# A decoder block in split fp32 on one core: residual tiles asked for earlier, a sum weighted ahead of its norm factor, conditioning sums moved one step on

## Chip, cores and metric

The kernel runs on one core of one Trainium2 chip. The metric is device microseconds of one execution, input in HBM to output in HBM.

## What is computed

One hybrid decoder block on x (1 x 1024 x 1024, float32). The reference, cut to the part that the change touches:

```python
ada = c_act @ w_ada[l] + b_ada[l]
sh1, sc1, gt1, sh2, sc2, gt2 = [a[:, None, :] for a in jnp.split(ada, 6, axis=-1)]
...
y = jax.nn.sigmoid(g_attn) * a + jax.nn.sigmoid(g_conv) * cv
x = x + gt1 * (y @ w_out[l])

h2 = rmsnorm(x, norm2_g[l]) * (1.0 + sc2) + sh2
fg, fu = jnp.split(h2 @ w_ffn_in[l], 2, axis=-1)
x = x + gt2 * ((jax.nn.silu(fg) * fu) @ w_ffn_out[l])
return rmsnorm(x, final_g)
```

## The kernel before

Activations are kept transposed, 128 channels on the partitions, in tiles of 128 x 1024 tokens, split into two token halves of 512 (`HB`). Every float32 operand of a matmul is split into a high part (rounded, written by ScalarE) and a low part (source minus high, made by VectorE), and a product is three matmuls: high x high, high x low, low x high. Three stages matter here.

**Output projection** (`wo`, L1116, 16 steps: eight channel tiles of the first token half, then eight of the second). Each step splits the next weight (`wh_wo` on ScalarE, `wl_wo` on VectorE, called through `low`), runs 24 matmuls into a bank, adds the result, weighted, to the residual tile `x1_m` on VectorE, stores that half to `x1_d` from POOL's queue (L1136), and squares it for the second norm. Beside this, VectorE makes the conditioning columns (`ada_step`, L272): a row tile of `w_ada` is fetched by SP (L269) into one of two buffers, multiplied by the condition vector and summed into one column of `cols` by a custom instruction. `AW` says how many are done in which step. Here a planner orders the instructions of TensorE, VectorE and ScalarE; behind the last step `in_order` fixes the program's own order.

**Transition into the feed-forward input.** The feed-forward products use Strassen's scheme: seven products per pair of hidden tiles (`Pair.PRODUCTS`), whose activations are A11, A12, A22 and the sums S1 to S4, and whose weights are B11, B22, B21, B12 and the differences T1 to T4. A11 and A12 are the first token half and are made during the projection. A21 and A22 are the second half and wait for the factor `rstd` of the second norm (`Norm2.stat`, L1076): ln and exp on ScalarE. For each of four channel tiles j, `scale1` (L1363) multiplies two tiles by weight and factor, adds them, has ScalarE write the high half of S1 with the two shifts added (`bsum`), and has ScalarE add the shift to each of the two tiles; `low1` makes the low half. `sums` makes S2 and leaves S3 in place, `sum4` makes S4, `blocks` splits S3 and A22. The first two pairs (`two`) run product by product side by side: 0, 5, 1, 2, 3, 4, 6; `both` (L1345) splits their weight blocks, and `evacuations` moves a finished bank out.

**Feed-forward output.** After the 22 pairs come `Group`s (L1268): the same seven products with three k-blocks each, whose activations (`gb`, 512 KB each) were stored to `gs_d` and come back through POOL's queue (`fetch_blocks`, L1466, issue L1476). Each product is added at once from its bank to the residual tile `x1r`, which `x1r()` (L1479, issue L1483) fetches from `x1_d` through SP's queue. SP's queue also carries the weight loads: L1176 for pairs, L1285 for Groups, two tiles each (`rawg` or `rawu`), and is served strictly in order. A slot for `gb` or `x1r` comes free when its last reader is done. The second product uses another bank than the first; the third uses the first's again.

```python
                if i == NFF - 1:
                    fetch_blocks(0, GP)
                    if p >= 5:
                        x1r()
```

## Time and profile before

| | us |
|---|---|
| runs (median, lowest, highest of 3) | 1387.37, 1385.5, 1387.46 |
| the profiled execution | 1386.32 |
| its span | 1384.6 |
| TensorE busy | 1333.0 |
| VectorE busy | 1063.5 |
| ScalarE busy | 637.0 |

The span is what the profile records of the execution; 1.7 us lie around it. The mean granted clock of TensorE is 0.994 of full speed. Times in the rows count from the start of the span. Busy time of TensorE is modelled from the starts of its matmuls, so gaps between them say more than its share.

### The profile page before, as it was taken

Reading aid. Unit: us, or ns where it says so; the run is one execution under the profiler, and the core shown is the slowest. Engines: PE = TensorE matmul, PEld = TensorE weight load, DVE = VectorE, ACT = ScalarE, POOL = GpSimd, SP = SyncE. Lnnn points to the kernel's source line nnn. Section 1 sums busy time; section 2 is a strip of 40 time slices with the busy share of each in tenths; the row PEclk is TensorE's granted clock in tenths of the full one; section 3 lists DMA queues with packets and bytes.
Section 4 is the critical chain, followed back from the end, with each engine's and each line's share of the span. In section 5 each row is a group of like instructions: output and inputs, shape, how many; then the busy total and the mean of one; then the engine's idle time right before and its main releaser. Section 6 shows DMA issues by size and latency. Waiting matters only on the chain.

```text
span 1384.6 us, 16471 instructions
## 1 busy us (share of the span) xinstructions
PE 1333.0 (96%) x6070; PEld 1090.8 (79%) x6070; DVE 1063.5 (77%) x1698; ACT 637.0 (46%) x1079; POOL 102.5 (7%) x181
## 2 busy tenths in 40 slices
PE   7899999999999999999997999999999997999997
PEld 5678887877788887788775888888888886888886
DVE  6847688889989897796789577877777765777764
ACT  5536667675611113732476454444444441222346
POOL 0000000000000000000100011111000031112004
PEclk9999999999999999999999999999999999999999
DMA  8610010100111122428721255554544499577213
GB/s 287 210 31 31 32 46 16 47 16 31 46 46 49 43 76 91 138 91 312 261 81 68 85 182 183 167 167 154 173 145 151 153 323 408 167 283 286 98 31 123
DMA packets 58899, 184.43 MB, mean 133 GB/s; under 512 B 6425, under 2 KB 11457, under 8 KB 58818
## 3 DMA queue, kind: packets, MB, share of 16 engines
q1 hardware_dynamic: 38242, 110.49, 24.3%
q0 software_dynamic: 20000, 72.36, 14.7%
q8 instruction: 48, 0.79, 0.2%
q10 hardware_dynamic: 576, 0.52, 0.1%
q14 instruction: 33, 0.27, 0.1%
HBM read 139.83 MB, written 43.52 MB: 132 GB/s over the span
## 4 chain that ended last, share of the span: by engine, by line
PE 77%; DVE 10%; ACT 6%; DMA 5%; issue 2%; SPq 0%; POOL 0%; DVEq 0%; ACTq 0%; POOLq 0%
PE fx L113 22%; PE fz L113 11%; PE proj L113 8%; PE ga L113 5%; PE fy L113 5%; PE gc L113 4%; PE wo L125 3%; PE oa L113 3%; PE oc L125 3%; PE fo L125 3%; DMA ada<-in_w_ada 2%; PE vacc L125 2%; PE sc L113 2%; PE av L113 2%; DMA gb<-gs_d 1%
## 5 line engine op out<-in xcount | busy, mean ns | idle before, releaser
L113 ACT ACTIVATE wbp<-tt 128x512 fp32r<-128x512 f32 (+1 forms) x75 | 43.9, 586 | 156.8 <-DVE tt L113 151.0
L113 DVE SCALAR_TENSOR_TENSOR cacc<-u,vec,cacc 128x1022 f32<-128x1022 f32 (+28 forms) x87 | 110.2, 1267 | 2.2
L113 PE MATMUL proj<-hhi,wh_in 128*128 128x512 f32 x239 | 98.3, 411 | 1.7 <-DVE kl L125 1.7
L113 PE MATMUL proj<-hhi,wl_in 128*128 128x512 f32 x240 | 93.9, 391 | 0.0
L113 PE MATMUL proj<-hlo,wh_in 128*128 128x512 f32 x240 | 93.6, 390 | 0.0
L113 ACT ACTIVATE wb<-tt 128x512 fp32r<-128x512 f32 (+1 forms) x59 | 35.4, 602 | 93.3 <-DVE tt L113 86.5
L113 PE MATMUL fx<-A,wb 128*128 128x512 f32 x299 | 70.9, 391 | 2.8 <-DVE g L113 2.8
L113 PE MATMUL fx<-S,wbp 128*128 128x512 f32 x276 | 67.1, 391 | 1.4 <-DVE S L113 1.3
L113 PEld LDWEIGHTS fx<-A,wb 128*128 128x128 f32 x299 | 56.0, 188 | 15.3 <-issue 3.7
L113 PE MATMUL fz<-S,wbp 128*128 128x512 f32 x276 | 66.5, 390 | 1.5 <-ACT S L113 1.3
L113 PE MATMUL fx<-gb,wbp 128*128 128x512 f32 x270 | 66.0, 390 | 0.3 <-DMA gb<-gs_d 0.3
L113 PE MATMUL fz<-S,wb 128*128 128x512 f32 x252 | 61.0, 390 | 1.6 <-DVE S L113 1.6
L113 PEld LDWEIGHTS fx<-S,wbp 128*128 128x128 f32 x276 | 51.6, 188 | 13.5 <-DVE S L113 2.5
L113 PE MATMUL fx<-S,wb 128*128 128x512 f32 x252 | 60.8, 390 | 1.4 <-DVE S L113 1.3
L113 PEld LDWEIGHTS fz<-S,wbp 128*128 128x128 f32 x276 | 51.7, 188 | 12.9 <-ACT S L113 1.7
L113 PEld LDWEIGHTS fx<-gb,wbp 128*128 128x128 f32 x270 | 50.5, 188 | 11.4 <-DMA gb<-gs_d 0.9
L125 ACT ACTIVATE e<-sc,mn 128x512 f32<-128x512 f32 (+7 forms) x64 | 47.2, 739 | 26.8 <-DVE mn L125 25.8
L113 DVE SCALAR_TENSOR_TENSOR x1r<-fx,cols,x1r 128x512 f32<-128x512 f32 x48 | 36.0, 750 | 30.2 <-PE fx L113 20.9
L113 PEld LDWEIGHTS fz<-S,wb 128*128 128x128 f32 x252 | 47.1, 188 | 12.2 <-DVE S L113 2.4
L113 PEld LDWEIGHTS fx<-S,wb 128*128 128x128 f32 x252 | 47.2, 188 | 11.9 <-DVE S L113 1.6
L113 DVE TENSOR_TENSOR wbp<-tt,wbp 128x512 fp32r<-128x512 f32 (+1 forms) x75 | 47.0, 628 | 11.7 <-ACT wbp L113 11.6
L113 PEld LDWEIGHTS proj<-hhi,wh_in 128*128 128x128 f32 x239 | 45.0, 188 | 11.1 <-issue 3.6
(354 smaller groups left out, 3603.8 us busy)
## 6 DMA issues: line engine op xcount, KB each, us to landing
gb<-gs_d POOLq DMA_DIRECT2D x57, 512.0 KB, 9.8
gs_d<-gstw POOLq DMA_DIRECT2D x36, 512.0 KB, 3.5
ada<-in_w_ada SPq DMA_DIRECT2D x32, 512.0 KB, 4.2
gs_d<-gst POOLq DMA_DIRECT2D x27, 512.0 KB, 4.3
rawu<-in_w_fi SPq DMA_DIRECT2D x22, 512.0 KB, 3.6
rawg<-in_w_fi SPq DMA_DIRECT2D x22, 512.0 KB, 4.5
adac<-in_w_ada SPq DMA_DIRECT2D x16, 512.0 KB, 5.2
wr_wo<-in_w_out SPq DMA_DIRECT2D x16, 512.0 KB, 5.0
```

Source lines behind the costliest of these rows:

```text
L113: self.last = f(*args, **kw)
L125: self.last = self.chain(f, *args, **kw) if self.chain else f(*args, **kw)
```

## The change

1. In the last pair, two x1r tiles are requested in the step of its first product, ahead of the rest of the first Group's `gb` blocks, of which that step asks for one and not three; before, they were requested in the steps of products 5 and 6.
2. S1 is formed from terms that are weighted before the factor is known: ScalarE weights A22's tile in place (`weigh22`: two tiles in the last projection step, two after the factor's instructions), VectorE adds the weighted A21 (`weigh1`: j = 0, 1 ahead of the factor). After the factor one multiplication per j remains ahead of the high half (`scale1`). S2 comes in one instruction from the sum, S3 in two from the unscaled tile, A22 in one multiplication by the factor, with the shift added on ScalarE (`sum22`) and again in the low half (`low22`). The T3 and T4 differences and the loads of pairs 2 and 3 move ahead of the first product. The low halves of T3 and T4 are no longer made by VectorE: ScalarE writes minus the high half, and an accumulating transfer from POOL's queue adds the source. The evacuations of product 0 move behind S1, the first pair's evacuation of product 4 ahead of A22. The factor gets a slot of its own.
3. The conditioning sums of a projection step are called in the next step, behind the low part of the next weight.

```diff
-                self.r = rstd_from([st], 1.0 / D, self.last)[0]
+                self.r = rstd_from([st], 1.0 / D, self.last, None if self.one else slot)[0]
...
             low()
+            if i:
+                ada_step(fx[0], AW[(i - 1) // KD][(i - 1) % KD], OCH)
             ps = bank("wo")
...
             norms[hf].add(m)
-            ada_step(fx[0], AW[hf][m], OCH)
             if hf:
                 for j in range(WA[m], WA[m + 1]):
                     apply0(j)
+            if i == 2 * KD - 1:
+                for j in range(KH - 2):
+                    weigh22(j)
...
-            def low(self, part):
+            def low(self, part, dma=False):
                 w, src = part
                 n = self.n
+                if dma:
+
+                    A.activation(w[:, n:2 * n], w[:, :n].bitcast(F32), AF.Copy, scale=-1.0)
+                    G.dma_start(w[:, n:2 * n], src, accum_op=ALU.add)
+                    return
...
+        def weigh22(j):
+
+            a22s.append(x1[KH + j][:, HB:])
+            A.activation(a22s[j], a22s[j], AF.Copy, scale=col(4, KH + j))
+
+        def weigh1(j):
+
+            if j % 2 == 0:
+                wide.append(slot(f"s1_{j}"))
+            sums1.append(wide[-1][:, hf_sl(j % 2)])
+            V.scalar_tensor_tensor(out=sums1[j], in0=x1[j][:, HB:], scalar=col(4, j), in1=a22s[j], op0=ALU.mult,
+                                   op1=ALU.add)
+
         def scale1(j):
-
-            for m in (j, KH + j):
-                norms[1].scale(m)
+            if j >= KH - 2:
+                weigh1(j)
+            t = sums1[j]
+            V.tensor_tensor(out=t, in0=t, in1=norms[1].r, op=ALU.mult)
             acts["S1"][j] = slot(f"S1_{j}", F32R)
-            t = sums1[j] = two[j % 2].t[:, HB:]
-            V.tensor_tensor(out=t, in0=x1[j][:, HB:], in1=x1[KH + j][:, HB:], op=ALU.add)
             A.activation(acts["S1"][j][:, :HB], t, AF.Identity, bias=bsum[:, j:j + 1])
-            for m in (j, KH + j):
-                norms[1].shift(m)
...
+        def sum2(j):
+
+            t = sums1[j]
+            V.scalar_tensor_tensor(out=t, in0=t, scalar=bsum[:, j:j + 1], in1=x1[j][:, :HB], op0=ALU.add,
+                                   op1=ALU.subtract)
+            high("S2", j, t)
+
+        def sum3(j):
+
+            norms[1].scale(j)
+            a21 = x1[j][:, HB:]
+            V.scalar_tensor_tensor(out=a21, in0=x1[j][:, :HB], scalar=col(3, j), in1=a21, op0=ALU.subtract,
+                                   op1=ALU.subtract)
+            high("S3", j, a21)
+
+        def sum22(j):
+            t = a22s[j]
+            V.tensor_tensor(out=t, in0=t, in1=norms[1].r, op=ALU.mult)
+            acts["A22"][j] = slot(f"A22_{j}", F32R)
+            A.activation(acts["A22"][j][:, :HB], t, AF.Identity, bias=col(3, KH + j))
...
         both(6, 7, 8, 9)
+        for j in range(KH - 2):
+            weigh1(j)
+        for t in ("T3", "T4"):
+            for g in two:
+                g.source(t)
+        pairs[2].load()
+        pairs[3].load()
         two[0].product(0)
         norms[1].stat()
+        for j in range(KH - 2, KH):
+            weigh22(j)
         two[1].product(0)
-        evacuations(0)
...
         staged(scale1, low1)
+        both(10, 11, dma=True)
+        evacuations(0)
         products(1)
         new_block("S2")
-        staged(sums, lambda j: low("S2", j, x1[j][:, :HB]))
+        staged(sum2, lambda j: low("S2", j, sums1[j]))
...
+        both(12, 13, dma=True)
         evacuations(2)
         products(3)
...
-        both(12, 13)
-        blocks("A22", lambda j: x1[KH + j][:, HB:])
-        evacuations(4)
+        two[0].evacuate(4)
+        new_block("A22")
+        staged(sum22, low22)
+        two[1].evacuate(4)
...
                 if i == NFF - 1:
-                    fetch_blocks(0, GP)
-                    if p >= 5:
+                    if p == 0:
+
                         x1r()
+                        x1r()
+                    fetch_blocks(0, GP if p else 1)
```

What this moves, at three places. First SP's queue around the last pair and the first Group, before:

```order
L1285 DMA rawg<-in_w_fo 128x768 x2
L1285 DMA rawu<-in_w_fo 128x768 x2
L1285 DMA rawg<-in_w_fo 128x768
L1483 DMA x1r_8893<-x_d 128x1024
L1483 DMA x1r_8911<-x_d 128x1024
L1483 DMA x1r_8973<-x_d 128x1024
L1483 DMA x1r_9005<-x_d 128x1024
L1285 DMA rawg<-in_w_fo 128x768
```

and now:

```order
L1294 DMA rawg<-in_w_fo 128x768 x2
L1294 DMA rawu<-in_w_fo 128x768
L1524 DMA x1r_8773<-x_d 128x1024
L1524 DMA x1r_8775<-x_d 128x1024
L1294 DMA rawu<-in_w_fo 128x768
L1294 DMA rawg<-in_w_fo 128x768 x2
L1524 DMA x1r_8979<-x_d 128x1024
L1524 DMA x1r_9011<-x_d 128x1024
```

Two x1r requests stand between the two `rawu` loads now, ahead of the `rawg` loads behind which all four stood; the other two stand behind the second of those.

Second VectorE around the factor (`wbp` are weight blocks, `small_78` holds the summed shifts, `cols_90` the weights and shifts), before:

```order
L113 TENSOR_TENSOR wbp_5576<-rawg_5497,wbp_5576 128x512
L113 TENSOR_TENSOR wbp_5578<-rawu_5501,wbp_5578 128x512
L113 SCALAR_TENSOR_TENSOR x1_0_4878<-x1_0_4878,cols_90,rstd_5601 128x512
L113 SCALAR_TENSOR_TENSOR x1_4_5037<-x1_4_5037,cols_90,rstd_5601 128x512
L113 TENSOR_TENSOR tt_5515<-x1_0_4878,x1_4_5037 128x512
L113 SCALAR_TENSOR_TENSOR x1_1_4919<-x1_1_4919,cols_90,rstd_5601 128x512
L113 SCALAR_TENSOR_TENSOR x1_5_5075<-x1_5_5075,cols_90,rstd_5601 128x512
L113 TENSOR_TENSOR tt_5520<-x1_1_4919,x1_5_5075 128x512
L113 SCALAR_TENSOR_TENSOR S1_0_5649<-tt_5515,small_78,S1_0_5649 128x512
```

and now:

```order
L113 TENSOR_TENSOR wbp_5578<-rawg_5497,wbp_5578 128x512
L113 TENSOR_TENSOR wbp_5580<-rawu_5501,wbp_5580 128x512
L113 SCALAR_TENSOR_TENSOR s1_0_5586<-x1_0_4878,cols_90,x1_4_5033 128x512
L113 SCALAR_TENSOR_TENSOR s1_0_5586<-x1_1_4915,cols_90,x1_5_5075 128x512
L113 TENSOR_TENSOR tt_5515<-rawg_5497 128x512
L113 TENSOR_TENSOR tt_5520<-rawu_5501 128x512
L113 TENSOR_TENSOR tt_5515<-rawg_5495,tt_5515 128x512
L113 TENSOR_TENSOR tt_5520<-rawu_5499,tt_5520 128x512
L113 TENSOR_TENSOR s1_0_5586<-s1_0_5586,rstd_5618 128x512 x2
L113 SCALAR_TENSOR_TENSOR S1_0_5663<-s1_0_5586,small_78,S1_0_5663 128x512
L113 SCALAR_TENSOR_TENSOR s1_2_5669<-x1_2_4957,cols_90,x1_6_5113 128x512
L113 TENSOR_TENSOR s1_2_5669<-s1_2_5669,rstd_5618 128x512
```

Two weighted sums and the four T3/T4 differences stand ahead of the first instruction that reads the factor; behind it, each S1 tile has one multiplication by the factor where three instructions stood.

Third ScalarE near the end of the projection (`x_4` and `x_6` are residual tiles, `wh_wo` the last weight's high half), before:

```order
L125 ACTIVATE A_0_5456<-x_4_5037 128x512
L125 ACTIVATE A_1_5556<-x_5_5075 128x512
L125 ACTIVATE sq<-x_4_5037 128x512
L125 ACTIVATE x_6_5136<-x_6_5136,cols 128x512
L125 ACTIVATE wh_wo_5461<-wr_wo_5459 128x1024
L125 ACTIVATE wb<-rawg 128x512
L125 ACTIVATE sq<-x_5_5075 128x512
L125 ACTIVATE wb<-rawu 128x512
```

and now:

```order
L125 ACTIVATE A_0_5456<-x_4_5033 128x512
L125 ACTIVATE A_1_5556<-x_5_5075 128x512
L125 ACTIVATE sq<-x_4_5033 128x512
L125 ACTIVATE x_4_5033<-x_4_5033,cols 128x512
L125 ACTIVATE x_6_5113<-x_6_5113,cols 128x512
L125 ACTIVATE wh_wo_5461<-wr_wo_5459 128x1024
L125 ACTIVATE wb<-rawg 128x512
L125 ACTIVATE sq<-x_5_5075 128x512
```

The weighing of x_4's second half, `x_4_5033<-x_4_5033,cols`, now stands ahead of the shift of x_6 and the last weight's high half.

## Rows read from the trace of the kernel before

**Rows 1.** Page, section 1: busy time of each engine.

```profile
PE 1333.0 (96%) x6070; PEld 1090.8 (79%) x6070; DVE 1063.5 (77%) x1698; ACT 637.0 (46%) x1079; POOL 102.5 (7%) x181
```

**Rows 2.** Windows: start:end, length, busy us of PE, PEld, DVE, ACT, POOL, PEclk, DMA share, GB/s.

```profile
712.00:745.00 33.00, 28.55 (x114) 20.52 (x113) 28.71 (x45) 23.33 (x36) 0.54 (x1) 1.00 0.02 9
745.00:760.00 15.00, 10.76 (x45) 8.07 (x44) 14.62 (x24) 9.49 (x17) 0.13 (x1) 1.00 0.41 140
...
1146.00:1160.00 14.00, 6.24 (x22) 4.77 (x21) 3.25 (x7) 0.94 (x2) 3.77 (x7) 0.76 1.08 408
```

**Rows 3.** Waits of PE, 600 to 1250: waited for, us, times, longest.

```profile
PE fx L113 <- issue: 7.8, 1, 7.8
PE fx L113 <- DVE g L113: 2.8, 1, 2.8
...
PE wo L125 <- DVE wl_wo L125: 2.1, 2, 1.3
```

**Rows 4.** Timeline of PE, first Group: start, us, engine line op, tiles [idle before <-releaser].

```profile
1147.39 1.52 PE L113 MATMUL fz<-gb,wbp 128*128 128x512 f32 x6
1156.67 3.63 PE L113 MATMUL fx<-gb,wb 128*128 128x512 f32 x9 [7.76 <-issue]
1160.14 2.22 PE L113 MATMUL fz<-gb,wb 128*128 128x512 f32 x9
...
1166.29 3.56 PE L113 MATMUL fx<-gb,wbp 128*128 128x512 f32 x15
```

**Rows 5.** Timeline of DVE, 1130 to 1164.

```profile
1145.94 0.55 DVE L113 TENSOR_TENSOR tt<-rawg 128x384 f32<-128x384 f32 x1
1155.82 0.75 DVE L113 SCALAR_TENSOR_TENSOR x1r<-fx,cols,x1r 128x512 f32<-128x512 f32 x1 [9.32 <-DMA x1r<-x_d]
```

**Rows 6.** Timeline of SP's DMA issues, 1110 to 1175.

```profile
1146.56 0.33 SPq L1285 DMA_DIRECT2D rawg<-in_w_fo  x1
1146.98 1.81 SPq L1483 DMA_DIRECT2D x1r<-x_d  x4
1160.22 0.33 SPq L1285 DMA_DIRECT2D rawg<-in_w_fo  x1
```

**Rows 7.** Timeline of POOL's DMA issues, 1100 to 1165.

```profile
1144.96 0.54 POOL L1476 DMA_DIRECT2D gb<-gs_d  x1 [0.71 <-PE fx L113]
...
1153.80 0.54 POOL L1476 DMA_DIRECT2D gb<-gs_d  x1 [1.78 <-DMA gb<-gs_d]
1156.43 0.54 POOL L1476 DMA_DIRECT2D gb<-gs_d  x1 [2.09 <-DMA gb<-gs_d]
```

**Rows 8.** Timeline of DVE, 645 to 765, at the transition.

```profile
719.47 1.41 DVE L113 SCALAR_TENSOR_TENSOR x<-x,cols,rstd 128x512 f32<-128x512 f32 x2 [3.51 <-ACT rstd L113]
...
748.04 1.28 DVE L113 TENSOR_TENSOR wb<-tt,wb 128x512 fp32r<-128x512 f32 x2
...
754.91 2.68 DVE L113 TENSOR_TENSOR A<-x,A 128x512 fp32r<-128x512 f32 x4
```

**Rows 9.** Timeline of ACT, 692 to 765.

```profile
700.39 0.72 ACT L125 ACTIVATE x<-x,cols 128x512 f32<-128x512 f32 x1 [2.48 <-DVE x L125]
```

**Rows 10.** Timeline of PE, 712 to 760, start of product 6.

```profile
758.33 1.85 PE L113 MATMUL fx<-A,wb 128*128 128x512 f32 x7 [2.85 <-DVE g L113]
```

**Rows 11.** Timeline of POOL, 640 to 765.

```profile
697.05 0.54 POOL L1136 DMA_DIRECT2D x_d<-x  x1 [5.59 <-DVE x L125]
...
759.87 0.54 POOL L1266 DMA_DIRECT2D g_d<-g  x1 [45.48 <-DVE g L113]
```

**Rows 12.** Tile x_d, 600 to 760: landing of its stores.

```profile
DMA to landing us min/median/max: 2.2/4.3/6.8
```

**Rows 13.** DMA issues, 1144 to 1165: KB each, median us to landing.

```profile
gb<-gs_d POOLq DMA_DIRECT2D x7, 512.0 KB, 17.6
```

**Rows 14.** Timeline of DVE, output projection.

```profile
662.02 1.28 DVE L125 CUSTOM_DVE_ANT_0 ada<-ada,crow,bada 128x1024 f32<-128x1024 f32 x1 [1.57 <-DMA ada<-in_w_ada]
...
665.70 1.22 DVE L125 TENSOR_TENSOR wl_wo<-wr_wo,wh_wo 128x1024 fp32r<-128x1024 f32 x1
```

More of the change, by code (lines that the diff above doesn't have):

```diff
@@ L1343, in prepare, with both @@
                 order[n][0].prepare(order[n][1])
-        def both(*ns):
+        def both(*ns, dma=False):
             parts = [(order[n][0], order[n][0].high(order[n][1])) for n in ns]
             for g, part in parts:
-                g.low(part)
+                g.low(part, dma)
         def staged(*stages):
@@ L1359, in new_block @@
             acts[name] = [None] * KH
-        sums1 = {}
+        wide, sums1, a22s = [], [], []
+        def weigh22(j):
[7 more added lines that the diff above has]
+                                   op1=ALU.add)
         def scale1(j):
-            for m in (j, KH + j):
-                norms[1].scale(m)
+            if j >= KH - 2:
+                weigh1(j)
+            t = sums1[j]
+            V.tensor_tensor(out=t, in0=t, in1=norms[1].r, op=ALU.mult)
             acts["S1"][j] = slot(f"S1_{j}", F32R)
-            t = sums1[j] = two[j % 2].t[:, HB:]
-            V.tensor_tensor(out=t, in0=x1[j][:, HB:], in1=x1[KH + j][:, HB:], op=ALU.add)
             A.activation(acts["S1"][j][:, :HB], t, AF.Identity, bias=bsum[:, j:j + 1])
-            for m in (j, KH + j):
-                norms[1].shift(m)
         def low1(j):
@@ L1376, in low1, with low22 @@
             V.scalar_tensor_tensor(out=t[:, HB:], in0=sums1[j], scalar=bsum[:, j:j + 1],
+                                   in1=t[:, :HB].bitcast(F32), op0=ALU.add, op1=ALU.subtract)
+        def sum2(j):
[14 more added lines that the diff above has]
+            A.activation(acts["A22"][j][:, :HB], t, AF.Identity, bias=col(3, KH + j))
+        def low22(j):
+            t = acts["A22"][j]
+            V.scalar_tensor_tensor(out=t[:, HB:], in0=a22s[j], scalar=col(3, KH + j),
                                    in1=t[:, :HB].bitcast(F32), op0=ALU.add, op1=ALU.subtract)
@@ L1385, in low @@
             V.tensor_tensor(out=t[:, HB:], in0=src, in1=t[:, :HB].bitcast(F32), op=ALU.subtract)
-        def sums(j):
-            a11, a21, a22 = x1[j][:, :HB], x1[j][:, HB:], x1[KH + j][:, HB:]
-            V.tensor_tensor(out=a21, in0=a11, in1=a21, op=ALU.subtract)
-            V.tensor_tensor(out=a11, in0=a22, in1=a21, op=ALU.subtract)
-            high("S2", j, a11)
         def sum4(j):
             a12 = x1[KH + j][:, :HB]
-            V.tensor_tensor(out=a12, in0=a12, in1=x1[j][:, :HB], op=ALU.subtract)
+            V.tensor_tensor(out=a12, in0=a12, in1=sums1[j], op=ALU.subtract)
             high("S4", j, a12)
-        def blocks(name, get):
-            new_block(name)
-            staged(lambda j: high(name, j, get(j)), lambda j: low(name, j, get(j)))
         jobs += [(oc, m, Weights(w_oc[m:m + 2], D, f"oc{m}")) for m in range(0, KD, 2)]
@@ L1438, in tile_hybrid_block @@
         staged(sum4, lambda j: low("S4", j, x1[KH + j][:, :HB]))
+        both(12, 13, dma=True)
         evacuations(2)
         products(3)
-        for t in ("T3", "T4"):
-            for g in two:
-                g.source(t)
-        pairs[2].load()
-        pairs[3].load()
-        both(10, 11)
-        blocks("S3", lambda j: x1[j][:, HB:])
+        new_block("S3")
+        staged(sum3, lambda j: low("S3", j, x1[j][:, HB:]))
         evacuations(3)
```

## Prediction

> **What bounds the kernel now.** I read the page's busy times first: TensorE is busy 96% of the span [rows 1], so at most some 50 us are to be had, and only where TensorE stands still. The windows show where some of that is: 712 to 760 holds 8.7 us (33.0 - 28.55 and 15.0 - 10.76), and 1146 to 1160 holds 7.8 us at a granted clock of 0.76 [rows 2]. The list of TensorE's waits names the largest pieces: 7.8 us in one piece at the end of the pair loop, 2.8 us for a VectorE `g` at the transition, and 2.1 us for the low half of an output-projection weight [rows 3]. The change has one part for each of the three places, and I cost them apart.
>
> **Part 1, x1r ahead.** After the second product of the first Group, TensorE stands still for 7.76 us [rows 4]. The page calls that "issue", but VectorE tells the cause: its first `x1r` update, which empties the bank of the first product, sat idle 9.32 us until the x1r transfer landed, and TensorE went on 0.85 us after that update began (1155.82 and 1156.67) [rows 4, 5]. The transfer was late because SP asked for it late: its queue is in order, the `rawg` load ahead of it was waiting for VectorE's last read of that buffer at 1145.94, and x1r0 to x1r3 followed at 1146.98 [rows 5, 6], into DMA engines that moved 408 GB/s [rows 2]. [...] Together 7.8 + 1.4 = 9.2 us.
>
> The change asks for x1r0 and x1r1 one product after the last pair begins, about 20 us earlier on SP, between the two `rawu` loads. They wait only for a slot. So the update finds its tile, and the 9.2 us go. What is late next is the stored-block stream. POOL issues one `gb` of 512 KB as another lands. Near the end two issues stand 2.63 us apart (1153.80, 1156.43) [rows 7], each waiting for a landing, because SP's x1r tiles share the engines; at 408 GB/s [rows 2] a tile alone would take 512 KB / 408 = 1.28 us. The set's last tile is requested at 1144.96 [rows 7]. The last three tiles (A22) land by these spacings near 1153.3, 1155.9 and 1158.7: the issue at 1156.43 follows the second of them by half a microsecond, and the third is one spacing on. The A22 product starts at 1166.29 now [rows 4], so without the stop at 1166.3 - 9.2 = 1157.1, and wants its third tile 1.4 us later, at 1158.5. There is no room left. Two x1r tiles ahead of the stream push it back by up to 2 x 1.28 = 2.6 us; what the stream wins back is that SP is quiet from about 1148 until the second `rawg`, which leaves at 1160.22 now [rows 6] and about 1151 then: some two microseconds at the full instead of half rate, one tile, 2.6 us at half rate. Bounds for the new stop: 0 and 4.2 us (the full push and 1.6 us for x1r2 and x1r3, which now come in right then). I take 2.0. The third and fourth x1r tiles, and the Group's own loads behind them, have several products in hand, so I cost them at nothing; if that cover goes, it shows as waits of `x1r` on VectorE after 1160. POOL's shorter first batch (one tile instead of three) costs nothing, as its issues there wait for landings anyway. **Net: 9.2 - 2.0 = 7.2 us**, between 5.0 and 9.2.
>
> [...]
>
> **Part 2, the transition.** VectorE is the chain here: from the first operation after the factor `rstd` (719.47, after 3.51 us of idling for it) to the end of the last A22 low half (754.91 + 2.68 = 757.59) it does 12 three-operand and 46 two-operand instructions. At 1.41 / 2 = 0.70 and 1.28 / 2 = 0.64 us [rows 8] that is 37.8 of 38.1 us: no slack. After the change the same stretch holds 22 and 31 (one of the first pair's product-4 evacuations now in it): 15.4 + 19.8 = 35.2, so 2.6 us less. The two weighted sums and four T3/T4 differences, 1.4 + 2.6 = 4.0 us, go into the idle 3.51 us; the half microsecond over delays nothing that ScalarE's factor does not delay anyway. The removed T3 and T4 low halves return as four ScalarE copies (an activation of this size is 0.72 us [rows 9]; ScalarE is idle 30% of this stretch [rows 2] and loses eight shifts of that kind) and four POOL accumulating transfers.
>
> Behind VectorE, product 6 now starts at 758.33 because the bank is emptied after all A22 work [rows 10]. With the first pair's evacuation ahead of A22, its twelve matmuls run under the A22 lows, and only the last three follow the last low. A matmul is about 0.225 us (15 in 3.56 against 9 in 2.22 [rows 4]), so 9 x 0.225 = 2.0 us more. Against it, that evacuation makes VectorE wait for product 4, whose twelve matmuls end some 2.7 us after the last S3 low, with three two-operand instructions (1.9 us) in between: 0.8 us lost. Gross 2.6 + 2.0 - 0.8 = 3.8.
>
> One side effect speaks against it. ScalarE's weighing of x1_4 stands ahead of the shift of x1_6 and the last weight split. It overwrites the tile, so it must wait until the store issued at 697.05 [rows 11] has landed; stores there take 2.2 to 6.8 us, median 4.3 [rows 12], so until about 701.4. The shift ran at 700.39 [rows 9]; it would run near 702, and VectorE, busy to the end of the stage, would carry that 1.6 us into the factor. TensorE has product 5 in hand but not all of it is free: I take 1.3. Handovers between ScalarE and VectorE that such a sum leaves out take another 0.5. **Net: 3.8 - 1.3 - 0.5 = 2.0 us**, between -2 (the store at its 6.8, nothing gained) and 6 (no shift, and the S1 stops gone).
>
> The accumulating transfers have no row. The near one is the 256 KB store, 2.2 to 6.8 us [rows 12]; the far one a `gb` in the full stream, 17.6 [rows 13]. POOL does nothing from the last store to 759.87 [rows 11] and the engines move 9 GB/s to 745 [rows 2], so it is nearest to the quiet store: I take 4.3. T3's two leave near 730 (after S1's ScalarE work); T3's lows were made at 748.04 [rows 8], so some 15 us are in hand. T4's leave near 743 and are wanted when the A22 work at 754.91 [rows 8] is: some 10.5 us in hand. Cost: nothing; from 10.5 us on, each microsecond is one.
>
> **Part 3, the conditioning sums.** In the output projection VectorE waits for conditioning rows (1.57 us before the sum at 662.02), and the weight's low half behind them starts at 665.70 [rows 14]; TensorE lost 2.1 us to such lows in two places [rows 3]. The sum is moved one step on, behind the next low half. The planner's order changes little: one sum fewer ahead of one evacuation, two ahead of the last. I take 0.8 of the 2.1, between -1 and 2.1.
>
> **Sum.** 7.2 + 2.0 + 0.8 = 10.0. The profiled execution took 1386.32 us, so 1376.3; the median shown is 1387.37, 1.05 above it, so **1377.4 us** for a median.
>
> **Rivals.**
> (a) The stored blocks become the bound: Part 1 gives only 5.0. For it: no room at the A22 product. Against: SP's quiet interval. Then 1387.4 - 5.0 - 2.8 = 1379.6.
> (b) The transition gives nothing or loses 2, since ScalarE's wait for the store reaches the factor: 1387.4 - 7.2 - 0.8 + 1 = about 1380.4; with (a), 1383.
> (c) The transition gives its full 6 (the stops between S1 and S4 close as well): 1373.4.
> (d) Slower: the accumulating transfers come late. POOL makes them while VectorE never pauses; if they got through only when VectorE rests, T3's lows would land near 762 instead of before 745, and product 4 would wait 14 to 17 us with everything behind it: 1377.4 + 15 = about 1392. It decides from 10.5 us of landing on and is slower than before from 20.5. Against it: x1 stores issued by POOL beside a busy VectorE landed in 2.2 to 6.8 us [rows 12].
> [...]
> (e) Part 1 does not do what it says: the two requests sit on SP for a slot until the old time, and only Parts 2 and 3 count: 1384.6.
>
> **Numbers.** About 0.2% of the time, 2.8 us, is what a measurement can tell from no change. Chances: the forecast 0.42, (a) 0.18, (b) 0.15, (c) 0.14, (d) 0.05, (e) 0.06. Below 1384.6 lie the forecast, (a), (c), nearly all of (b): faster 0.85. Same 0.09: (e) and what of (b) meets (a). Slower 0.06: (d), and mishaps of (b) and (e) together. The range reaches from (c) with some of Part 1's full 9.2 to (b) with (a) and a little over: 1371 to 1384.5, leaving out (d), (e) and part of (c).
>
> **What would show it.** Right: the first x1r issue near 1127 by the old clock and no VectorE wait for it; no "issue" stop and a granted clock of 1.0 around the first Group; a stop for DMA `gb` of 0 to 4 us at its seventh product; VectorE's first multiplication by the factor followed at once by S1's high half; the four accumulating transfers landing within 7 us; product 6's first matmul before the last A22 low. Wrong: a TensorE wait at products 4 or 6 for the accumulating transfers, a factor later by more than 2 us, or x1r requests still near 1147.

## The result, and the profile after

The changed kernel takes 1378.45 us (median of 6 runs, 1377.21 to 1381.22); before took 1386.01 us in the same comparison (6 runs, 1384.32 to 1387.46). The ratio is 0.9946, with a 95% interval of 0.9932 to 0.9960: 7.5 us less, between 5.5 and 9.4. The forecast was 1377.4.

| profiled execution, us | before | after |
|---|---|---|
| its time | 1386.32 | 1377.21 |
| span | 1384.6 | 1375.4 |
| TensorE busy | 1333.0 | 1334.2 |
| VectorE busy | 1063.5 | 1064.6 |
| ScalarE busy | 637.0 | 636.6 |

The two spans differ by 9.2 us, but not all of that is the change. The next table cuts each profiled execution at the starts of five matmuls: the first of the output projection, the first of the feed-forward input, the third pair's first (172 matmuls on), the first Group's first that reads a `gb` block, and the one 81 matmuls behind that. Columns are the times between them; the first runs from the span's start and the last to the last matmul. Each row is one execution. (The runs of the experiments stand in it too; each is told below.)

| kernel | ahead | projection | transition | pairs | first Group | rest |
|---|---|---|---|---|---|---|
| before | 621.07 | 91.09 | 51.71 | 380.80 | 27.73 | 203.08 |
| after | 618.88 | 90.33 | 51.07 | 380.80 | 22.61 | 202.41 |
| p1_alone | 618.59 | 89.67 | 51.73 | 380.80 | 21.66 | 203.73 |
| p2_alone | 621.50 | 91.63 | 51.54 | 380.80 | 28.61 | 202.38 |
| p3_alone | 619.04 | 91.69 | 53.47 | 380.80 | 27.91 | 202.94 |
| x1r_pool | 619.91 | 90.82 | 51.43 | 380.80 | 19.13 | 202.36 |
| weigh_late | 621.25 | 91.17 | 49.93 | 380.80 | 22.77 | 202.53 |
| lows_ve | 618.64 | 91.63 | 50.98 | 380.80 | 22.05 | 203.44 |
| s3_from_s2 | 620.11 | 91.45 | 49.12 | 380.80 | 23.91 | 202.63 |
| best | 620.72 | 93.12 | 47.63 | 380.80 | 19.86 | 202.74 |
| p4_side | 619.02 | 90.36 | 52.01 | 380.80 | 24.77 | 202.84 |
| best_side | 619.31 | 91.15 | 45.46 | 380.80 | 19.35 | 202.77 |

Read it by columns. "Ahead" is the same code in all twelve, and ranges over 2.9 us; so 2.2 of the 9.2 us are one execution against another. The projection is the same code in before and p1_alone, 1.4 us apart, and in weigh_late, best and best_side, 2.0 us apart. The transition is the same code in before, p1_alone and p3_alone: 51.71, 51.73 and 53.47. Of the 1.8 us between them, 1.6 are matmuls at a lower clock: behind a stop of much the same length, 2.85 and 2.81 us, product 6 ran at full clock in before (granted 1.00 from 756 to 762) and not in p3_alone (0.72 there),

```profile
758.33 8.43 PE L113 MATMUL fx<-A,wb 128*128 128x512 f32 x36 [2.85 <-DVE g L113]
```

```profile
757.06 10.03 PE L113 MATMUL fx<-A,wb 128*128 128x512 f32 x36 [2.81 <-DVE g L113]
```

so that one trace sizes a gain in the transition to no better than some 1.8 us. "First Group" holds the change: 27.73 to 22.61, 5.1 us less, against 81 x 0.2267 = 18.4 us if nothing stopped (0.2267: the starts of nine matmuls in this Group at a granted clock of 1.00, 1149.23 to 1151.27 in the changed kernel, over nine). The transition got 0.6 us shorter.

**Part 1 in the trace.** SP's DMA issues of the changed kernel (start, length of the issue):

```profile
1122.91 1.01 SPq L1524 DMA_DIRECT2D x1r<-x_d  x2
...
1142.96 4.46 SPq L1294 DMA_DIRECT2D rawg<-in_w_fo  x2
1147.52 0.86 SPq L1524 DMA_DIRECT2D x1r<-x_d  x2
```

The first two x1r requests leave at 1122.91, 24 us ahead of where they left [rows 6], and VectorE's first two updates wait for TensorE alone:

```profile
1143.32 0.75 DVE L113 SCALAR_TENSOR_TENSOR x1r<-fx,cols,x1r 128x512 f32<-128x512 f32 x1 [0.41 <-PE fx L113]
...
1145.36 0.75 DVE L113 SCALAR_TENSOR_TENSOR x1r<-fz,cols,x1r 128x512 f32<-128x512 f32 x1 [0.82 <-PE fz L113]
```

No row of [rows 5]'s kind (9.32 us for an x1r transfer) is left. TensorE's waits from 600 to 1250, and its timeline at the first Group's seventh product, show what is late in its place:

```profile
PE fx L113 <- DMA gb<-gs_d: 2.0, 2, 1.5
...
PE wo L125 <- DVE wl_wo L125: 1.7, 2, 0.9
```

```profile
1153.31 0.84 PE L113 MATMUL fx<-gb,wbp 128*128 128x512 f32 x3
1154.68 0.96 PE L113 MATMUL fx<-gb,wbp 128*128 128x512 f32 x3 [0.53 <-DMA gb<-gs_d]
1157.17 3.87 PE L113 MATMUL fx<-gb,wbp 128*128 128x512 f32 x9 [1.52 <-DMA gb<-gs_d]
1160.83 0.94 PE L113 MATMUL fx<-gbw,wbp 128*128 128x512 f32 x3
```

The product has nine matmuls in three pieces; its second and third block came late, by 0.5 and 1.5 us in the bracket's count, and the nine matmuls from 1157.17 on (the last three of the product and six of the next Group's first) took 3.66 us to the next start instead of 2.04, at a granted clock of 0.50 from 1158 to 1160. From 1153.31 to 1160.83 are 15 matmuls, 3.4 us at full clock; they took 7.5, so 4.1 us went back. The windows agree (columns as in [rows 2]):

```profile
712.00:745.00 33.00, 29.23 (x117) 21.21 (x115) 30.62 (x49) 25.01 (x41) 4.11 (x5) 0.99 0.38 104
745.00:760.00 15.00, 13.97 (x43) 9.63 (x44) 13.59 (x21) 6.41 (x11) 0.56 (x1) 0.79 0.03 14
...
1146.00:1160.00 14.00, 11.95 (x47) 9.13 (x47) 8.42 (x16) 2.40 (x5) 3.86 (x8) 0.91 1.09 410
```

**Part 2 in the trace.** In these windows 745 to 760 has a clock of 0.79 where it had 1.00 [rows 2]. The weighing on ScalarE waits for the store, as foretold (the start and length, and in the bracket the wait and what ended it):

```profile
698.70 1.34 ACT L125 ACTIVATE x<-x,cols 128x512 f32<-128x512 f32 x2 [3.75 <-DMA x_d<-x]
```

It stands 3.75 us for the store of x1. The row holds two activations of one shape: the weighing and, right behind it, the shift of x1_6, which ran at 700.39 before [rows 9]. VectorE from the factor to A22's last low half:

```profile
718.12 1.29 DVE L113 TENSOR_TENSOR s<-s,rstd 128x512 f32<-128x512 f32 x2
...
728.15 0.69 DVE L113 TENSOR_TENSOR S<-s,S 128x512 fp32r<-128x512 f32 x1 [1.49 <-ACT S L113]
...
749.52 0.69 DVE L113 TENSOR_TENSOR g<-keptb,g 128x512 f32<-128x512 f32 x1 [0.46 <-ACT g L113]
...
755.35 1.41 DVE L113 SCALAR_TENSOR_TENSOR A<-x,cols,A 128x512 fp32r<-128x512 f32 x2 [0.19 <-ACT A L113]
```

and TensorE, from its first feed-forward matmul to product 6:

```profile
709.21 0.39 PE L110 MATMUL fx<-A,wb 128*128 128x512 f32 x1
...
745.02 1.65 PE L113 MATMUL fx<-S,wb 128*128 128x512 f32 x3 [1.09 <-DVE S L113]
747.07 6.18 PE L113 MATMUL fx<-S,wb 128*128 128x512 f32 x17 [0.40 <-DVE S L113]
753.09 1.24 PE L113 MATMUL fx<-A,wb 128*128 128x512 f32 x4
...
756.16 7.00 PE L113 MATMUL fx<-A,wb 128*128 128x512 f32 x29 [0.29 <-DVE A L113]
```

The first multiplication by the factor starts 718.12 - 709.21 = 8.91 us after the first feed-forward matmul. Before, that matmul was

```profile
712.17 0.39 PE L110 MATMUL fx<-A,wb 128*128 128x512 f32 x1
```

and the distance 719.47 - 712.17 = 7.30 [rows 8]: it is 1.6 us later. From there to the last A22 low half are 38.6 us (to 755.35 + 1.41), where there were 38.1 [rows 8]: half a microsecond more, with 2.9 us of idling where there was next to none (the list of VectorE's waits has 3.5 us for the factor and 0.2 for one `g` before). Behind the last low half, 3.5 us pass to the third pair's first matmul and not 6.3: 2.8 us less. 1.6 + 0.5 - 2.8 = -0.7 is the 0.6 of the table. The accumulating transfers, T3's and T4's (in the second column of times the span of their issues, below it issue to landing):

```profile
L1211 POOL DMA_DIRECT2D wb<-tt x4: 860/1038/1232, 726.4 to 741.1; - x4
...
DMA to landing us min/median/max: 3.2/3.9/4.5
```

**Part 3 in the trace.** 90.33 us of projection against 91.09, which the spread of the same code does not tell from nothing; TensorE waited 1.7 us for `wl_wo` where it was 2.1 [rows 3]. In the table the nine projections with Part 3 average 91.3 us, the three without it 90.8.

### The profile page after: what moved, and what is told of

Its sections match the earlier page's. It is cut to its first block, busy times and chain, and to the rows that moved or that the text cites. A ratio compares the mean times of both kernels' runs of the same rounds, so it can differ in the third digit from the quotient of the medians.

```text
span 1375.4 us, 16487 instructions
## 1 busy us (share of the span) xinstructions
PE 1334.2 (97%) x6070; PEld 1091.5 (79%) x6070; DVE 1064.6 (77%) x1698; ACT 636.6 (46%) x1079; POOL 106.2 (8%) x185
## 4 chain that ended last, share of the span: by engine, by line
PE 76%; DVE 11%; ACT 7%; DMA 4%; issue 2%; SPq 0%; DVEq 0%; ACTq 0%
PE fx L113 22%; PE fz L113 11%; PE proj L113 8%; PE ga L113 6%; PE fy L113 5%; PE gc L113 4%; PE oa L113 3%; PE oc L125 3%; PE fo L125 3%; DMA ada<-in_w_ada 2%; PE wo L125 2%; PE sc L113 2%; PE vacc L125 2%; PE av L113 2%; DMA gb<-gs_d 1%
## 5 line engine op out<-in xcount | busy, mean ns | idle before, releaser
L113 PE MATMUL fx<-S,wb 128*128 128x512 f32 x252 | 64.1, 403 | 2.2 <-DVE S L113 1.7
```

What stands on the lines that cost most here:

```text
L113: self.last = f(*args, **kw)
```

## The experiments

All stand on the kernel before or the changed one and were compared with the kernel before on the same chip, the first four, the next four and the last two together. Three theories were at stake: that the three parts simply add; that what came back in Part 1 is the transfer engines shared between queues; and, for Part 2, whether VectorE's chain, the wait for the store, or the slow clock took its gain.

### p1_alone: Part 1 on the kernel before

```diff
                 if i == NFF - 1:
-                    fetch_blocks(0, GP)
-                    if p >= 5:
+                    if p == 0:
                         x1r()
+                        x1r()
+                    fetch_blocks(0, GP if p else 1)
```

> The kernel before with Part 1 alone (x1r0 and x1r1 requested in the last pair's first product). Theory (the parts add, and Part 1 carries most): the 7.8 us stop and the slow nine matmuls behind it go, 9.2 us; back come a stop for the late A22 blocks at the seventh product of the first Group (2.2 us of waiting in the trace of the changed kernel) and about 1.9 us of slow matmuls behind it; net 5 to 6 us, so about 1380.5 where before is 1386. Rival (the parts need each other: the earlier part of the change has to bring the last pair forward for the requests to help): under 3 us. Rival (the late blocks come from Part 2's other timing, not from x1r): no block stop, 9 us gained, about 1377.

Measured: 1382.18 us (12 runs, 1377.07 to 1389.57, the widest of all), ratio 0.9972, interval 0.9956 to 0.9988; so 3.9 us less, between 1.7 and 6.1. In the trace, which is of the fastest of the twelve (1377.07), the first Group is 27.73 - 21.66 = 6.1 us shorter. The stops for blocks are there without Part 2:

```profile
1154.99 0.96 PE L113 MATMUL fx<-gb,wbp 128*128 128x512 f32 x3 [1.13 <-DMA gb<-gs_d]
1157.51 2.37 PE L113 MATMUL fx<-gb,wbp 128*128 128x512 f32 x9 [1.56 <-DMA gb<-gs_d]
1159.72 0.85 PE L113 MATMUL fx<-gbw,wbp 128*128 128x512 f32 x3
```

So they come from Part 1. Here the nine matmuls from 1157.51 took 2.21 us to the next start: after stops of 1.1 and 1.6 us (a little more than in the changed kernel) the clock was still full (1.00 from 1154 to 1162, where the changed kernel has 0.79), and so the slow matmuls do not come with every such stop. That Part 1 carries most and brings the stops stands, and the rival without stops falls. The rival of under 3 us falls by the trace; the interval alone, from 1.7 us on, would leave it, and the size stays open between that and the trace's 6 us.

### p2_alone: Part 2 on the kernel before

The changed kernel with the hunks of the last pair and of `ada_step` taken back:

```diff
             low()
-            if i:
-                ada_step(fx[0], AW[(i - 1) // KD][(i - 1) % KD], OCH)
             ps = bank("wo")
...
+            ada_step(fx[0], AW[hf][m], OCH)
...
-                    if p == 0:
-                        x1r()
-                        x1r()
-                    fetch_blocks(0, GP if p else 1)
+                    fetch_blocks(0, GP)
+                    if p >= 5:
+                        x1r()
```

> The kernel before with Part 2 alone (S1 from terms weighted ahead of the factor, with the accumulating transfers). The traces of before and after have 54.4 and 53.8 us from the first feed-forward matmul to the third pair's first. Theory (the instructions saved on VectorE are lost again to a clock that falls behind the short stops of product 4): the stage is again 53.5 to 54.2 us, the time 0 to 1 us below before, the granted clock under 0.9 between product 4 and product 6. Rival (the slow clock in the one trace was chance): the stage is 51 to 52.5 us with a clock of 1.0, the time 2 to 3 us below before.

Measured: 1383.33 us (12 runs), ratio 0.9986, interval 0.9974 to 0.9998: 1.9 us less, between 0.3 and 3.6. The transition takes 51.54 us, 0.2 less than before, and again with the slow clock. (The expectation counted the stage 12 matmuls further, hence its 54.4 and 53.8; by that count it is 54.26 here, just above the theory's 54.2 and well above the rival's 52.5.)

```profile
742.00:756.00 14.00, 11.81 (x37) 8.14 (x36) 13.15 (x21) 7.47 (x14) 1.75 (x2) 0.76 0.21 38
```

The stage gains as little as the theory said, and the slow clock is no accident: in 742 to 756 it is 0.76 to 0.88 in all seven kernels that have Part 2 and run product 4 pair by pair (the changed one, this one, x1r_pool, weigh_late, lows_ve, s3_from_s2, best), and 1.00 in the three without Part 2 (before, p1_alone, p3_alone). That it costs the gain is not shown by this, and the run of p4_side below speaks against it. The trace, of an execution 3.8 us above the median, has only 0.2 us of the median's 1.9 in the transition. Against the transition of p3_alone, 53.47 us with before's code, it would be 1.9. So the runs leave Part 2's size open between 0.3 and 3.6 us.

### p3_alone: Part 3 on the kernel before

```diff
             low()
+            if i:
+                ada_step(fx[0], AW[(i - 1) // KD][(i - 1) % KD], OCH)
             ps = bank("wo")
...
-            ada_step(fx[0], AW[hf][m], OCH)
```

> The kernel before with Part 3 alone (conditioning sums behind the next low half). The projection, from its first matmul to the first feed-forward matmul, is 90.9 us before and 90.2 after, 87.05 of it matmuls. Theory (fetches of the conditioning rows bound the sums, so moving the sums hardly helps): 90.0 to 90.6 us here, the time 0.3 to 0.9 us below before, which the runs can't tell from no change. Rival (the sums ahead of the low half were the cause): under 88.5 us.

Measured: 1386.13 us (12 runs), ratio 1.0003, interval 0.9993 to 1.0013: no difference, and the projection takes 91.69 us. The rival falls. The theory's 0.3 to 0.9 us lies within the interval (1.0 us better to 1.8 worse), and so does nothing; its projection of 90.0 to 90.6 us did not come out in this trace. The three parts alone sum to 2.8 + 1.4 - 0.3 = 3.9 thousandths where the whole has 5.4; each has 1.0 to 1.6 of uncertainty, so that they add is allowed and not proved.

### x1r_pool: the next two x1r tiles behind the blocks

```diff
-                nc.sync.dma_start(x1[-1], x1_d[len(x1) - 1])
+                (G if len(x1) in (3, 4) else nc.sync).dma_start(x1[-1], x1_d[len(x1) - 1])
```

> The changed kernel with x1r2 and x1r3 asked for from POOL's queue, behind the first Group's blocks, and not from SP's. Theory (the A22 blocks are late because x1r2 and x1r3 take half of the transfer engines from 1147.5 on): the two stops for blocks at the first Group's seventh product (0.5 and 1.5 us) and the slow matmuls behind them go, up to 4.1 us, so 1374.5 to 1376 where the changed kernel is 1378.5. Rival (x1r0 and x1r1, ahead of the stream, push it back for good): the stops stay at 1.5 us or more, the time within 1 us of the changed kernel. Rival (x1r2 and x1r3 come too late from there): VectorE waits for x1r near 1162, and the time is 1378 to 1382.

Measured: 1375.09 us (6 runs, 1374.35 to 1375.91), ratio 0.9924, interval 0.9908 to 0.9940; 3.4 us below the changed kernel's median. POOL issues x1r2 and x1r3 after the last block of the first Group:

```profile
1146.85 0.54 POOL L1524 DMA_DIRECT2D x1r<-x_d  x1 [0.74 <-DMA gb<-gs_d]
1148.10 0.54 POOL L1524 DMA_DIRECT2D x1r<-x_d  x1 [0.71 <-DMA gb<-gs_d]
```

and the seventh product runs through almost unstopped:

```profile
1155.19 1.69 PE L113 MATMUL fx<-gb,wbp 128*128 128x512 f32 x6
1157.18 2.34 PE L113 MATMUL fx<-gb,wbp 128*128 128x512 f32 x9 [0.29 <-DMA gb<-gs_d]
1159.36 0.84 PE L113 MATMUL fx<-gbw,wbp 128*128 128x512 f32 x3
```

15 matmuls at full clock take 3.4 us and 4.2 pass between 1155.19 and 1159.36, so 0.8 us is lost in all, against 4.1. So the late blocks came from x1r2 and x1r3 taking their share from 1147.5 on, as the theory had it; x1r0 and x1r1 ahead of the stream can account for no more than the 0.8. The table bears it out: the first Group takes 21.66 to 24.77 us in the six kernels with Part 1 that keep x1r2 and x1r3 on SP's queue, and 19.13 to 19.86 in the three that have them on POOL's. VectorE does not wait for x1r2: the two transfers landed within 12.1 us of their requests, and its next update of an x1r tile, at 1160.24, waits for TensorE alone.

### weigh_late: the first two weighings behind the shift of x1_7

```diff
-            if i == 2 * KD - 1:
-                for j in range(KH - 2):
-                    weigh22(j)
...
+        for j in range(KH - 2):
+            weigh22(j)
         both(6, 7, 8, 9)
```

> The changed kernel with the first two weighings on ScalarE (x1_4, x1_5) moved behind the shift of x1_7, so that nothing of the projection waits for the stores of x1. The stage from the first feed-forward matmul to the third pair's first is 51.1 us in the changed kernel (51.7 before), and VectorE's first multiplication by the factor starts 8.9 us after the first feed-forward matmul (7.3 before). Theory (the wait for the store, 3.75 us on ScalarE, is carried by VectorE into the factor): the multiplication starts 7.2 to 7.8 us in, the stage is 49.6 to 50.3 us. Rival (the later factor comes from the longer ScalarE and VectorE work alone): start and stage as in the changed kernel within 0.3 us.

Measured: 1378.61 us (6 runs), ratio 0.9950, interval 0.9932 to 0.9969, no difference from the changed kernel that such runs can tell. The trace tells it: ScalarE's shift of x1_6 waits for VectorE only, as before the change,

```profile
700.67 0.72 ACT L125 ACTIVATE x<-x,cols 128x512 f32<-128x512 f32 x1 [2.48 <-DVE x L125]
```

and VectorE's first multiplication by the factor

```profile
720.18 1.28 DVE L113 TENSOR_TENSOR s<-s,rstd 128x512 f32<-128x512 f32 x2
```

is 7.76 us behind the first feed-forward matmul (712.42), 1.15 less than in the changed kernel; the transition takes 49.93 us, 1.14 less. The theory stands: without the wait for the store the factor comes 1.15 us earlier, and the transition is shorter by as much. Not all of ScalarE's 3.75 us is the store's price, since the same place waits 2.48 us for VectorE without it.

### lows_ve: T3's and T4's low halves on VectorE again

```diff
-        both(10, 11, dma=True)
+        both(10, 11)
...
-        both(12, 13, dma=True)
+        both(12, 13)
```

> The changed kernel with the four low halves of T3 and T4 made by VectorE again, without the ScalarE copies and the accumulating transfers (which landed in 3.2 to 4.5 us). Theory (the transfers are free and VectorE sets the stage): four more VectorE instructions of 0.6 us, the stage 1.5 to 2.4 us longer than the 51.1 of the changed kernel. Rival (ScalarE's copies ahead of S2's high halves cost as much as they save, VectorE idles 1.5 us there): the stage within 0.7 us of it.

Measured: 1380.22 us (6 runs), ratio 0.9963, interval 0.9947 to 0.9978. The transition takes 50.98 us, as in the changed kernel: the rival is right. VectorE's chain:

```profile
718.48 1.29 DVE L113 TENSOR_TENSOR s<-s,rstd 128x512 f32<-128x512 f32 x2
...
725.62 1.28 DVE L113 TENSOR_TENSOR wb<-tt,wb 128x512 fp32r<-128x512 f32 x2
...
756.32 1.42 DVE L113 SCALAR_TENSOR_TENSOR A<-x,cols,A 128x512 fp32r<-128x512 f32 x2 [0.19 <-ACT A L113]
```

Four more instructions, but no wait for S2's high half: from the factor to the last low half 39.3 us (718.48 to 757.74) where the changed kernel has 38.6. The transfers saved 0.6 us of the 2.4 that leave VectorE; most of the rest went into ScalarE's two extra copies ahead of S2, for which VectorE idled 1.49 us at 728.15. (The factor came 0.7 us earlier in this execution, which is why the stage does not show the 0.6.)

### s3_from_s2: S3 as A22 minus S2

```diff
-            norms[1].scale(j)
-            a21 = x1[j][:, HB:]
-            V.scalar_tensor_tensor(out=a21, in0=x1[j][:, :HB], scalar=col(3, j), in1=a21, op0=ALU.subtract,
-                                   op1=ALU.subtract)
+            t, a21 = a22s[j], x1[j][:, HB:]
+            V.tensor_tensor(out=t, in0=t, in1=norms[1].r, op=ALU.mult)
+            V.scalar_tensor_tensor(out=a21, in0=t, scalar=col(3, KH + j), in1=sums1[j], op0=ALU.add,
+                                   op1=ALU.subtract)
...
-            V.tensor_tensor(out=t, in0=t, in1=norms[1].r, op=ALU.mult)
             acts["A22"][j] = slot(f"A22_{j}", F32R)
...
-        evacuations(3)
         for g in two:
             g.product(4)
-        two[0].evacuate(4)
         new_block("A22")
         staged(sum22, low22)
+        two[0].evacuate(4)
+        evacuations(3)
         two[1].evacuate(4)
```

> The changed kernel with S3 formed as A22 minus S2 (one multiplication by the factor that A22 needs anyway, and one three-operand instruction), and A22's low halves right behind S3's, ahead of the evacuations of products 3 and 4. Four three-operand instructions fewer on VectorE, 2.8 us. Theory (VectorE sets the stage, and the slow clock comes with the stops in product 4 of the first pair, which the new order leaves): 48 to 49.5 us where the changed kernel has 51.1, the clock still under 0.9 in product 4. Rival (the slow matmuls set the stage from product 4 on): 50.5 us or more.

Measured: 1377.56 us (6 runs, 1372.21 to 1379.01), ratio 0.9935, interval 0.9915 to 0.9955; transition 49.12 us, 2.0 less. VectorE is through A22 at 753.0:

```profile
744.90 0.69 DVE L113 TENSOR_TENSOR S<-x,S 128x512 fp32r<-128x512 f32 x1 [0.70 <-ACT S L113]
...
750.29 2.74 DVE L113 SCALAR_TENSOR_TENSOR A<-x,cols,A 128x512 fp32r<-128x512 f32 x4
```

but product 4's last 17 matmuls took until 755.23, 5.6 us where 17 at full clock take 3.9:

```profile
749.63 5.76 PE L113 MATMUL fx<-S,wb 128*128 128x512 f32 x17 [0.82 <-DVE S L113]
755.23 8.32 PE L113 MATMUL fx<-A,wb 128*128 128x512 f32 x36
```

Here TensorE at its lower clock (0.88 from 742 to 756, 1.00 from 756 to 764), and no longer VectorE, is what product 6 waits for. VectorE's idle of 0.70 us at 744.90 is for a high half that stands on ScalarE behind T4's copies, as S2's stood behind T3's.

### best: the four together

Edits of x1r_pool, weigh_late and s3_from_s2, and T3's high halves and copies between S1's high halves:

```diff
+            if j == 2:
+                early.extend((order[n][0], order[n][0].high(order[n][1])) for n in (10, 11))
+            if j == 3:
+                for g, part in early:
+                    g.low(part, True)
...
-        both(10, 11, dma=True)
```

> Everything together on the changed kernel: x1r2 and x1r3 on POOL's queue behind the first Group's blocks, the two weighings behind the shift of x1_7, S3 from A22 minus S2, and T3's high halves and copies in ScalarE's idle time between S1's high halves, which takes 2.1 us away from ahead of S2's. Theory (the gains add): the stage 46.5 to 48.5 us where the changed kernel has 51.1, 1375.1 less 2.5 to 4.5: 1370.5 to 1372.5. Rival (each gain uncovers the next wait): 1373.5 to 1375.

Measured: 1374.19 us (5 runs, 1370.49 to 1375.78), ratio 0.9916, interval 0.9898 to 0.9934. The transition takes 47.63 us, as the theory had it, and the time is the rival's. The profiled execution is the slowest of the five and has a projection of 93.12 us, the longest of all, with the code of weigh_late there (91.17); what made the median long, no run tells. VectorE is through A22 at 753.0, 31.4 us after the factor at 721.64 (38.6 in the changed kernel), and product 6 waits till 756.0 for product 4 at the slow clock:

```profile
750.27 2.74 DVE L113 SCALAR_TENSOR_TENSOR A<-x,cols,A 128x512 fp32r<-128x512 f32 x4
```

```profile
756.01 8.34 PE L113 MATMUL fx<-A,wb 128*128 128x512 f32 x36
```

```profile
742.00:756.00 14.00, 11.29 (x32) 7.45 (x31) 12.56 (x20) 8.40 (x15) 1.75 (x2) 0.76 0.21 38
```

### p4_side: product 4 of the two pairs side by side

```diff
-        for g in two:
-            g.product(4)
+        products(4)
         two[0].evacuate(4)
```

> The changed kernel with product 4 of the first two pairs run side by side (six matmuls for each S3 block that arrives, where the first pair's three ran alone and the second pair followed). In the changed kernel TensorE stands for 1.3 us between bursts of three there and then runs at the lower clock level until 751. Theory (the slow clock is what took Part 2's gain, and it comes from the thin stretch of product 4): the clock stays at 1.0 and the stage from the first feed-forward matmul to the third pair's is 48 to 49.5 us where the changed kernel has 51.1. Rival (VectorE's chain through A22 sets the stage, and TensorE would only wait for A22 if it came through product 4 sooner): 50.7 to 51.3 us whatever the clock does.

Measured: 1380.55 us (6 runs), ratio 0.9951, interval 0.9936 to 0.9967. The transition takes 52.01 us, 0.9 more than the changed kernel:

```profile
747.43 2.79 PE L113 MATMUL fx<-S,wb 128*128 128x512 f32 x11 [0.38 <-DVE S L113]
752.65 0.49 PE L113 MATMUL fx<-A,wb 128*128 128x512 f32 x1 [2.44 <-ACT A L113]
...
754.98 9.29 PE L113 MATMUL fx<-A,wb 128*128 128x512 f32 x32 [0.29 <-DVE A L113]
```

Product 4 came through at the full clock (the last 11 start within 2.4 us, and the granted clock is 0.96 from 742 to 756, with the first matmuls of product 6 in that stretch) and TensorE then stood 2.4 us for A22's high half; product 6 ran at the lower clock instead (0.85 from 756 to 764). VectorE's chain did not move: its last A22 low half,

```profile
755.72 1.42 DVE L113 SCALAR_TENSOR_TENSOR A<-x,cols,A 128x512 fp32r<-128x512 f32 x2 [0.19 <-ACT A L113]
```

ends 47.8 us after the first feed-forward matmul (709.38), and 47.6 us after it in the changed kernel. So in the changed kernel the slow stretch of product 4 lay in time that TensorE would have waited for A22 anyway. The rival is right, though the stage came out above its 51.3 us, by the slow matmuls of product 6: the clock did not take Part 2's gain, VectorE's chain did.

### best_side: the same on best

```diff
-        for g in two:
-            g.product(4)
+        products(4)
         new_block("A22")
```

> The kernel of the run called best with product 4 of the first two pairs side by side. There A22 is ready soon after S3, so that product 4's second half, 12 matmuls at the lower level, is what product 6 waits for. Theory (slow clock from the thin stretch): 45.5 to 46.5 us where best has 47.6, clock 1.0; about 1372.5. Rival (the clock falls all the same, from the stops ahead of it): 47 us or more.

Measured: 1369.33 us (4 runs, 1368.98 to 1370.03), ratio 0.9874, interval 0.9859 to 0.9889; transition 45.46 us. Where A22 is early, as in best, product 4 is what product 6 waits for, and there the clock counts. With product 4 at full clock product 6 starts at 750.36, and waits for VectorE, which empties product 4's bank behind A22:

```profile
749.54 0.68 DVE L113 TENSOR_TENSOR g<-fx,keptc 128x512 f32<-128x512 f32 x1
```

```profile
746.22 2.83 PE L113 MATMUL fx<-S,wb 128*128 128x512 f32 x11 [0.32 <-DVE S L113]
750.36 8.45 PE L113 MATMUL fx<-A,wb 128*128 128x512 f32 x36 [1.31 <-DVE g L113]
```

```profile
742.00:756.00 14.00, 11.80 (x49) 8.77 (x49) 13.12 (x21) 7.16 (x12) 0.56 (x1) 1.00 0.18 51
```

The clock is 1.00 here and 0.76 in the same window of best, and the stage 2.2 us shorter. The theory stands for the stage and the clock; the time came out 3 us below its 1372.5. The medians of best and best_side, of different comparisons, differ by 4.9 us, of which the stage explains 2.2. This kernel beats both: 9.1 us below the changed one by the medians of different comparisons, 17 below before.

## Why the prediction was right, and where its sizes were off

The forecast of 1377.4 us lies 1.1 below the median of 1378.45, and the direction and most of the mechanism came out. But its sum of 10.0 us lies outside the 5.5 to 9.4 that were measured, and its first two terms were too large by the table: 7.2 and 2.0 against 5.1 and 0.6. By the medians of the parts alone the first is too large (3.9, between 1.7 and 6.1), and the second is not told apart (1.9, between 0.3 and 3.6); the third, 0.8, is within the spread of the same code. That the absolute time came so near is in part luck: before itself took 1386.01 in this comparison, 1.4 less than the 1387.37 that the sum was set on. The 1379.6 of rival (a) lies about as near to the median as the forecast does, and its account of Part 1 is the better one.

**Part 1: 9.2 us away, 2.0 back, net 7.2.** The 9.2 are right: the 7.8 of it is the wait of 7.76 us and the 1.4 the difference of the nines behind it, 3.63 and 2.22 us [rows 4], at a granted clock of 0.50 from 1156 to 1158 and 0.61 from 1158 to 1160 in that trace; both are gone from the old place, and the requests left at 1122.91, which is 1126.5 on before's time axis, near the 1127 foretold. The stop for the A22 blocks was foretold at 2.0 and is 2.0 in the list of TensorE's waits above. The step left out of the new stop what its own first half counts for the old one, the slow matmuls behind it. In the changed kernel's trace 4.1 us came back with the slow matmuls, net 5.1 in the table. Rival (a), the blocks as the bound with 5.0 net, is therefore what this trace shows, though for another reason than the full push by x1r0 and x1r1; x1r_pool shows that the competition of x1r2 and x1r3 makes it, which the prediction had only in the upper bound (its "1.6 us for x1r2 and x1r3").

x1r0 and x1r1 alone cost TensorE little. The prediction's bound has them push the stream back by up to 2.6 us; in x1r_pool, where they leave early too (from 1124.8 on) and x1r2 and x1r3 come from POOL's own queue behind the blocks, 0.8 us is lost at the blocks in all, where it is 4.1 in the changed kernel.

**Part 2: 3.8 gross, 1.3 for the store, 0.5 for handovers, net 2.0.** Measured 0.2 to 0.6 in three traces of this code, against the trace of before with its transition at full clock. The store's wait cost 1.15 to 1.6, as put. The end of the chain gave 2.8, more than the 2.0 put. The step that failed is VectorE's chain: 2.6 less was foretold, less 0.8 and 0.5 for waits, so 1.3 less, and it is 0.5 more. The count of instructions was right (15.4 + 19.8 = 35.2; 38.6 less 2.9 of idling is 35.7), but waits came to 2.9 us and not 1.3 (the 0.5 for handovers had no row behind it). Half of that is one wait, 1.49 us: S2's high half stood on ScalarE behind T3's four copies and two evacuations. The copies were costed by ScalarE's idle share of the stage, 30%, and not by what stood behind them at that place.

**The accumulating transfers.** Taken at 4.3 us, landed in 3.2 to 4.5, never waited for: rival (d) did not happen, and its condition (10.5 us) was far. VectorE was busy for 30.62 of the 33 us from 712 to 745, in which all four were asked for (726.4 to 741.1).

**Part 3: 0.8 of 2.1.** p3_alone shows none (between 1.8 us worse and 1.0 better). The prediction saw that the order changes little; its 0.8 had no row behind it.

**The other rivals.** (b), the transition giving nothing, is what came out for Part 2 by the traces, without its loss of 2; the medians leave it open. (c) did not come out, though best_side shows that the stage had 6 us in it (51.71 to 45.46). (e) did not happen. The two profiled executions differ by 9.2 us only because 2.2 of "ahead", 0.8 of the projection and 0.7 of "rest" add to the change's own 5.1 and 0.6; "ahead" has no edit in it, and the 0.8 is within the spread of the same code.

## What to carry to other kernels

When a wait is removed by asking for data earlier, follow the queue that the request shares its engines with to its own next deadline, and put what is not urgent behind what is on the same queue: that was worth 3.4 us here, two thirds of what the early request itself gained in the trace. Price a stop of TensorE with the slow matmuls that can follow it, as a range and on both sides of the sum: here much the same stops were followed by 1.6 us of them in the changed kernel and by 0.2 in p1_alone. Work given to an idle engine is free only if nothing that the critical engine waits for stands behind it in that engine's order: here VectorE idled 1.49 us for S2's high half behind T3's copies on ScalarE.

## What the runs showed of the hardware that was not expected

- Whether the granted clock fell behind a stop was not told by the stop's length. Behind 2.8 us ahead of product 6, with the same code, the 36 matmuls took 8.43 us in before, 8.41 in p1_alone and 10.03 in p3_alone. In product 4 of the changed kernel, bursts of three matmuls with 0.4 to 1.1 us of waiting between them were followed by matmul starts 0.43 us apart until 751, at a granted clock of 0.50 from 746 to 750. With six matmuls to a burst product 4 ran at full clock (the last 11 in 2.79 us in p4_side and in 2.83 in best_side); product 6 behind it did so too in best_side, after a wait of 1.31 us (36 in 8.45 us), and did not in p4_side, after one of 2.44 (its last 32 in 9.29 us).
- After stops of much the same length for blocks, the matmuls behind them were slow in the changed kernel (nine in 3.66 us) and at full clock in p1_alone (nine in 2.21 us).
- An accumulating transfer of 256 KB (`wb<-tt`) occupied POOL 0.86 to 1.23 us at issue, where a plain transfer took 0.54, and landed in 3.2 to 4.5 us, where the plain store of that size took 2.2 to 6.8 in before [rows 12].
- Code that is the same in all kernels took 618.6 to 621.5 us up to the projection, from one execution to the next.
